# A two-layer image transformer on one core: the joint between the layers and the last steps are rebuilt

## The chip, the cores and the metric

The kernel runs on one core of one Trainium2 chip. A core has five engines that run side by side and wait for each other only through semaphores: PE (TensorE, matrix products into PSUM, with a separate queue for weight loads, PEld), DVE (VectorE), ACT (ScalarE), POOL (GpSimd) and SP (SyncE, which here issues most DMAs). The metric is the device time of one execution in microseconds (us); the median of several runs counts.

## The reference, cut to what matters

Two layers work on 256 tokens of `x` and 256 context tokens `ctx`, each of width 2048. Layer 0 is a Fourier branch, layer 1 an attention branch. Each layer normalises its input, modulates it, and adds a gated product back:

```python
for i in range(DEPTH):
    shift, scale, gate = split(silu(c) @ ada_w[i] + ada_b[i])
    h = rmsnorm(x, norm_g[i]) * (1 + scale) + shift
    hc = rmsnorm(xc, norm_g[i]) * (1 + scale_c) + shift_c
    y, yc = branch(h, hc)                 # Fourier, then attention
    x = x + gate * (y @ w_out[i])
    xc = xc + gate_c * (yc @ w_out[i])    # layer 0 only
return rmsnorm(x, final_g)
```

`rmsnorm(x, g)` is `x * rsqrt(mean(x*x) + 1e-6) * g`, the mean taken over the 2048 features of one token. So layer 1 can't begin before the squares of all features of layer 0's result are summed, and the output can't be written before those of layer 1's result are.

## The kernel before

Every large product is computed in three passes, because both operands are split into a high part (a rounded copy, made by ACT) and a low part (the difference, made by DVE): `split` (L61, L62) makes the parts, `half_split` applies it to half of a loaded weight block, and `mm3` (L74 to L76) issues high x high, high x low and low x high into the same PSUM bank. Weight blocks of 1 MB come in through three buffers (`raw`), and three pairs of split halves (`ws`) lie ready for PE. A scheduler orders each engine's instructions from a model of their times; `tc.issue_after(i)` only holds later instructions of the same engine behind instruction `i` in that order.

Within layer 0 the features lie on the partitions and the 512 tokens (256 of `x`, 256 of `ctx`) along the free axis. The last product of layer 0 runs over 32 steps, 16 for each half of the features, with all eight PSUM banks in use. In the last step of a half the banks are finished one by one, and `evac0` (L670 to L681) empties each: DVE adds the gated product to `x` (L674, two instructions), ACT squares the result (L677), and DVE adds the square to a running sum (L679). Of the 16 blocks of features the first 15 go into one sum and the last stays apart.

Then comes the joint, L705 to L736. PE turns the blocks by 128x128 transposes (`x1_turn`, L714), so that tokens lie on the partitions; ACT copies them out of PSUM (L716) and issues their DMA to a buffer in DRAM (L717), from which the end of the kernel fetches them. The sums over features are products with a column of ones (L731), two operands for each of four token blocks. `rsqrt` (L78 to L87) takes the root: DVE scales and adds epsilon (L82), GpSimd raises to the power of -0.5 (L83), and three DVE instructions do one Newton step (L84 to L86). `bcast_rows` (L97 to L101) spreads the four columns over all partitions with PE, and ACT copies the result out. Six turns stand ahead of the sums, two behind the broadcast. Layer 1 begins with the normalised, modulated blocks (L768 to L770) and the product with the key and value weights (`wkv`, L775), whose splits also go through L61 and L62.

At the end of layer 1 the output has four column blocks of 512 (`cb`) for two token blocks (`tb`). The last column block is computed with both token blocks side by side for five weight blocks; then token block 0 goes ahead with the last three, and token block 1's twelve steps are held back (`held`) and run last. `evac` (L1073 to L1081) multiplies a bank by the gate, adds `x` and has ACT square and sum it. `finish` (L1107 to L1119) adds the four partial sums, takes the root with `rsqrt`, scales the four column blocks (two on ACT, L1118, two on DVE, L1114 and L1116) and writes them out from SP (L1119).

## Time and profile before

| what | us |
|---|---|
| median of 3 runs | 1862.07 |
| lowest and highest | 1858.95 and 1866.89 |
| the profiled execution's own time | 1863.31 |
| its span in the profile | 1861.5 |
| last matmul of layer 0 ends, first matmul of layer 1 starts | 1029.98, 1040.88 |
| last matmul of the kernel ends | 1850.08 |

Times in the profile are counted from the start of the span. A timeline row gives start, duration, engine, line, operation, output and inputs with their shape, how many instructions are merged, and in brackets the idle time ahead of it with what ended it. Matmuls overlap each other, so the distance between two starts is their cost, not the duration of a row. One product with float32 operands stands as two passes in PE's counts.

### The profile page before, as it was taken

How to read it: one execution, taken by the hardware profiler on the slowest of the kernel's cores; microseconds unless marked ns; L12 is line 12 of the kernel's file. 1: busy time of each engine (PE TensorE's matmuls, PEld its weight loads, DVE VectorE, ACT ScalarE, POOL GpSimd, SP SyncE). 2: the span in 40 equal slices, each digit the busy share in tenths (PEclk: the TensorE clock that was granted, in tenths of full speed). 3: DMA queues.
4: the chain of work that ended last, by engine and by line, in shares of the span. 5: the costliest groups of instructions: out<-in, count | busy, mean ns of one | idle time of the engine just before them, and what ended most of it. 6: DMA issues, size and time to landing. Idle time of an engine off the chain costs nothing.

```text
span 1861.5 us, 26287 instructions
## 1 busy us (share of the span) xinstructions
PE 1824.5 (98%) x9953; PEld 1555.9 (84%) x9953; DVE 1412.0 (76%) x2406; ACT 976.5 (52%) x1713; POOL 158.7 (9%) x182
## 2 busy tenths in 40 slices
PE   7998999999999999999999999999999999999997
PEld 6658999998888888888888787888888888887886
DVE  5657999978897898578964825888878878887454
ACT  6445444444222243224222624888888888896343
POOL 0001000020000000000000001111220220300010
PEclk9999999999999999999999999999999999999999
DMA  7984565585766756654675324333333333434543
GB/s 314 362 355 148 196 209 197 188 287 204 299 259 228 277 197 256 257 216 165 228 265 215 114 94 147 123 135 132 118 120 130 136 117 133 159 136 181 186 176 136
DMA packets 63934, 362.74 MB, mean 195 GB/s; under 512 B 7744, under 2 KB 7888, under 8 KB 29504
## 3 DMA queue, kind: packets, MB, share of 16 engines
q1 hardware_dynamic: 52448, 326.67, 48.0%
q0 software_dynamic: 7472, 27.71, 4.0%
q10 hardware_dynamic: 3888, 6.69, 1.2%
q8 instruction: 78, 1.28, 0.3%
q14 instruction: 48, 0.39, 0.1%
HBM read 346.87 MB, written 14.16 MB: 194 GB/s over the span
## 4 chain that ended last, share of the span: by engine, by line
PE 93%; DVE 2%; DMA 2%; ACT 2%; issue 1%; POOL 0%; ACTq 0%; POOLq 0%; SPq 0%; DVEq 0%
PE ps L74 24%; PE ps L75 24%; PE ps L76 24%; PE ps L950 6%; PE ps L952 3%; PE ps L1006 3%; PE ps L1021 2%; PE ps L1020 2%; PE ps L986 2%; PE ps L987 1%; PE ps L254 1%; DMA m<-in_wm 1%; DMA raw<-in_awp 0%; DVE wl L62 0%; PE ps L236 0%
## 5 line engine op out<-in xcount | busy, mean ns | idle before, releaser
L61 ACT CAST wh<-raw 128x1024 fp32r<-128x1024 f32 x329 | 345.0, 1051 | 457.6 <-PE ps L75 348.6
L62 DVE TENSOR_TENSOR wl<-raw,wh 128x1024 fp32r<-128x1024 f32 x329 | 415.9, 1267 | 200.0 <-ACT wh L61 197.4
L75 PE MATMUL ps<-act,wh 128*128 128x512 f32 x928 | 361.0, 389 | 0.0
L74 PE MATMUL ps<-act,wh 128*128 128x512 f32 x928 | 357.9, 389 | 0.0
L76 PE MATMUL ps<-act,wl 128*128 128x512 f32 x928 | 356.6, 389 | 0.8 <-DVE wl L62 0.8
L76 PEld LDWEIGHTS ps<-act,wl 128*128 128x128 f32 x928 | 174.2, 188 | 37.3 <-DVE wl L62 1.2
L75 PEld LDWEIGHTS ps<-act,wh 128*128 128x128 f32 x928 | 174.2, 188 | 36.0
L74 PEld LDWEIGHTS ps<-act,wh 128*128 128x128 f32 x928 | 174.2, 188 | 35.9
L950 PE MATMUL ps<-h,wh 128*128 128x512 f32 x512 | 187.0, 400 | 0.0
L579 DVE CUSTOM_DVE_ANT_0 raw<-raw,cb 128x1024 f32<-128x1024 f32 x128 | 154.8, 1220 | 33.7 <-DMA raw<-in_adw 32.7
L579 DVE CUSTOM_DVE_ANT_0 junk<-raw,cb 128x1024 f32<-128x1024 f32 x96 | 117.1, 1220 | 29.4 <-DMA raw<-in_adw 16.1
L952 PE MATMUL ps<-h,wl 128*128 128x256 f32 x512 | 138.1, 280 | 0.0
L75 PE MATMUL ps<-wl,h 128*128 128x512 f32 x320 | 126.1, 394 | 1.5 <-DVE wl L62 1.5
L74 PE MATMUL ps<-wh,h 128*128 128x512 f32 x320 | 124.8, 398 | 0.2 <-ACT h L769 0.2
L76 PE MATMUL ps<-wh,h 128*128 128x512 f32 x320 | 124.5, 391 | 0.0
L950 PEld LDWEIGHTS ps<-h,wh 128*128 128x128 f32 x512 | 96.2, 188 | 19.0
L988 DVE CUSTOM_DVE_ANT_0 ps<-ps,mask,nsink 128x512 f32<-128x512 f32 x128 | 92.1, 754 | 12.3 <-PE ps L987 11.3
L991 ACT ACTIVATE p<-ps,mx 128x512 f32<-128x512 f32 x128 | 87.3, 687 | 24.8 <-DVE mx L988 24.2
L952 PEld LDWEIGHTS ps<-h,wl 128*128 128x128 f32 x512 | 96.8, 189 | 1.4
L62 DVE TENSOR_TENSOR pl<-ps,ph 128x512 fp32r<-128x512 f32 x128 | 83.7, 685 | 10.0 <-ACT ph L61 8.8
L996 ACT ACTIVATE p<-p,sm 128x512 f32<-128x512 f32 x128 | 85.4, 717 | 7.9 <-DVE sm L994 7.8
L75 PE MATMUL ps<-wl,ys 128*128 128x512 f32 x212 | 83.3, 393 | 0.0
(323 smaller groups left out, 3790.6 us busy)
## 6 DMA issues: line engine op xcount, KB each, us to landing
raw<-in_adw SPq DMA_DIRECT2D x64, 1024.0 KB, 5.1
raw<-in_wz SPq DMA_DIRECT2D x62, 1024.0 KB, 4.9
raw<-in_awp SPq DMA_DIRECT2D x32, 1024.0 KB, 8.0
raw<-in_wo SPq DMA_DIRECT2D x32, 1024.0 KB, 5.6
raw<-in_wq SPq DMA_DIRECT2D x32, 1024.0 KB, 4.8
raw<-in_wu SPq DMA_DIRECT2D x32, 1016.0 KB, 5.4
raw<-in_wo1b SPq DMA_DIRECT2D x16, 1024.0 KB, 4.9
act<-in_xT POOLq DMA_DIRECT2D x32, 256.0 KB, 5.2
```

What stands on the lines that cost most here:

```text
L61: S.copy(h, src)
L62: V.tensor_tensor(l, src, h.bitcast(F32), op=ALU.subtract)
L74: PE.matmul(o, wh, xh, start=start, stop=False)
L75: PE.matmul(o, wh, xl, start=False, stop=False)
L76: PE.matmul(o, wl, xh, start=False, stop=stop)
L579: V.tensor_tensor_reduce(junk if s == 0 and i < 3 else wf, wf, cb[:, s], 1.0, 0.0, ALU.mult, ALU.add, acc[:, i, kh, fg * 2 + f, s : s + 1])
L950: PE.matmul(o[0], wh[:, q], hx1[k], start=k == 0, stop=k == KT - 1)
L952: PE.matmul(o[0][:, 0:N], wl[:, q], hx1[k][:, 0:N], start=False, stop=False)
L988: V.tensor_tensor_reduce(o, o, mask[:, tb, :], -0.125, nsink[:, i : i + 1], ALU.add, ALU.min, mx[:, tb : tb + 1])
L991: S.activation(pt[:, tb, :], so[tb], AF.Exp, bias=mx[:, tb : tb + 1], scale=-1.0, accum_out=sm[:, tb : tb + 1])
L996: S.activation(pt[:, tb, :], pt[:, tb, :], AF.Copy, scale=sm[:, tb : tb + 1])
L1006: PE.transpose(o[:, (kt * 2 + tb) * P : (kt * 2 + tb + 1) * P], pt[:, tb, c : c + P], ident)
```

## The change

- The sums at the joint: the squares of the last two feature blocks of layer 0 are no longer added by DVE, but are two further operands of the product with ones. The square of block 13 is added behind the last evacuation. There are three operands for each of four token blocks instead of two.
- The root: `root` takes the square root on ACT and the reciprocal on DVE, then the same Newton step. `rsqrt` with GpSimd's power stays for layer 0's first norm. A one-element square root is issued at step 24 of layer 0's last product, and another one near the end, so that ACT holds its table.
- The turns: one group of two stands ahead of the sums, one between sums and broadcast, and two groups behind the broadcast; before it was three groups ahead and one behind.
- The first block of key and value weights: its first half is split at the last step of layer 0, its second half behind the first normalised block of layer 1.
- The end: the first three partial sums are added ahead of time (`known`), so that the root takes the last partial sum with the rest as its bias. Token block 1's last four steps are computed in two half banks of 256 columns, each emptied by itself (`part`); the full bank of its other steps is added to `x` meanwhile. The pieces are scaled and written in the order 2, 0, 3, 1, and the last piece of token block 1 is written from ACT's queue.

```diff
+    def root(pool, src, w, tag, bias=None):
+        v = pool.tile([P, w], F32, tag=tag + "v", name=tag + "v")
+        t = pool.tile([P, w], F32, tag=tag + "s", name=tag + "s")
+        r = pool.tile([P, w], F32, tag=tag + "r", name=tag + "r")
+        b = epsd if bias is None else bias
+        first = S.activation(t, src, AF.Sqrt, bias=b[:, 0:1], scale=1.0 / D).ins
+        V.tensor_scalar(v, src, 1.0 / D, EPS if bias is None else bias[:, 0:1], op0=ALU.mult, op1=ALU.add)
+        V.reciprocal(r, t)
+        newton(r, v, t)
+        return r, first
...
-            S.activation(t2, t, AF.Square)
-            if 0 < k < 15:
-                V.tensor_tensor(sqs[0], sqs[0], t2, op=ALU.add)
+            sq_end[0] = S.activation(t2, t, AF.Square).ins
+            if 0 < k < 14:
+                if k == 13:
+                    late.append(t2)
+                else:
+                    V.tensor_tensor(sqs[0], sqs[0], t2, op=ALU.add)
             else:
                 sqs.append(t2)
+            if k == 15:
+                with tc.issue_after(e):
+                    V.tensor_tensor(sqs[0], sqs[0], late[0], op=ALU.add)
...
+            if i == 31:
+                kv_raw = raw(a["wkv"][0])
+                kv_w = [half_split(kv_raw, 0)]
+            if i == 24:
+                S.activation(junk[:, 0:1], epsd, AF.Sqrt)
...
-    for c in range(3):
-        for tb in range(2):
-            x1_turn(tb, c)
+    turns(0, sq_end[0])
     r_bc1 = act()
     o = psum()
-    for t in range(4):
-        for i in range(2):
-            PE.matmul(o[:, t : t + 1], sqs[i][:, t * P : (t + 1) * P], ones[:, 0:1], start=i == 0, stop=i == 1)
-    r4 = rsqrt(const, o[:, 0:4], 4, "q")
-    bcast_rows(r4, r_bc1)
-    for tb in range(2):
-        x1_turn(tb, 3)
+    for i in (1, 2, 0):
+        for t in range(4):
+            with tc.issue_after(p_end[0]):
+                last = PE.matmul(o[:, t : t + 1], sqs[i][:, t * P : (t + 1) * P], ones[:, 0:1], start=i == 1 and t == 0, stop=i == 0 and t == 3).ins
+        p_end[0] = last
+    r4, rooted = root(const, o[:, 0:4], 4, "q")
+    turns(1, rooted, p_end[0])
+    with tc.issue_after(p_end[0]):
+        spread = bcast_rows(r4, r_bc1)
+    for c in (2, 3):
+        turns(c, p_end[0], spread)
...
+            def part(tb, j, o):
+                q, t, x = slice(1536 + j * 256, 1792 + j * 256), act()[:, 0:256], x2[tb][3][:, j * 256 : (j + 1) * 256]
+                V.tensor_tensor(t, o, gbc[:, q], op=ALU.mult)
+                V.tensor_tensor(x, x, t, op=ALU.add)
+                S.activation(t, x, AF.Square, accum_out=ss[:, 8 + j : 9 + j])
...
-            def finish(tb):
-                s2 = fp.tile([P, 1], F32, tag="s2", name="s2", bufs=2)
-                V.tensor_reduce(s2, ss[:, tb * 4 : tb * 4 + 4], axis=AX.X, op=ALU.add)
-                r = rsqrt(fp, s2, 1, f"f{tb}")
-                for c in (0, 3, 1, 2):
+            def finish(tb, col, base):
+                r, _ = root(fp, ss[:, col : col + 1], 1, f"f{tb}", base)
+                for c in (2, 0, 3, 1):
...
-                    nc.sync.dma_start(out[tb * P : (tb + 1) * P, c * 512 : (c + 1) * 512], t)
+                    (nc.scalar if tb and c == 1 else nc.sync).dma_start(out[tb * P : (tb + 1) * P, c * 512 : (c + 1) * 512], t)
...
-            finish(0)
-            for k, w in held:
+            base = [known(tb, 3, ss[:, tb * 4 : tb * 4 + 3], EPS) for tb in range(2)]
+            S.activation(ss[:, 9:10], epsd, AF.Sqrt)
+            finish(0, 3, base[0])
+            for k, w in held[:-4]:
                 step(k, 1, *w)
-            evac(1, 3, o[1])
-            finish(1)
+            t, x = act(), x2[1][3]
+            V.tensor_tensor(t, o[1], gbc[:, 1536:2048], op=ALU.mult)
+            V.tensor_tensor(x, x, t, op=ALU.add)
+            for j in range(2):
+                oh = psum()[:, 0:256]
+                for i, (k, (wh, wl)) in enumerate(held[-4:]):
+                    q = slice(j * 256, (j + 1) * 256)
+                    mm3(oh, yh[k][:, P : 2 * P], yh[k][:, N + P : 2 * N], wh[:, q], wl[:, q], i == 0, i == 3)
+                part(1, j, oh)
+                if j == 0:
+                    last = known(1, 1, ss[:, 8:9], base[1][:, 0:1])
+            finish(1, 9, last)
```

More of the change, by code (lines that the diff above doesn't have):

```diff
@@ L83, in rsqrt, with newton @@
         GP.tensor_tensor(r, v, mhalf[:, 0:w], op=ALU.pow)
+        newton(r, v, t)
+        return r
+    epsd = const.tile([P, 1], F32, name="epsd")
+    GP.memset(epsd, EPS)
+    def newton(r, v, t):
         V.tensor_tensor(t, r, r, op=ALU.mult)
@@ L86, in rsqrt @@
         V.scalar_tensor_tensor(r, t, 1.5, r, op0=ALU.add, op1=ALU.mult)
-        return r
+    def root(pool, src, w, tag, bias=None):
[6 more added lines that the diff above has]
+        V.reciprocal(r, t)
+        newton(r, v, t)
+        return r, first
     ident = const.tile([P, P], F32, name="ident")
@@ L100, in bcast_rows @@
             PE.matmul(o[:, t * P : (t + 1) * P], r4[:, t : t + 1].broadcast_to([P, P]), ident, start=True, stop=True)
-        S.copy(dst, o)
+        return S.copy(dst, o).ins
     gs0 = const.tile([P, KT, 2], F32, name="gs0")
@@ L673, in evac0 @@
                 q = slice(s * N, (s + 1) * N)
-                V.scalar_tensor_tensor(t[:, q], o[:, q], gt0[:, k, s : s + 1], t[:, q], op0=ALU.mult, op1=ALU.add)
+                e = V.scalar_tensor_tensor(t[:, q], o[:, q], gt0[:, k, s : s + 1], t[:, q], op0=ALU.mult, op1=ALU.add).ins
             x1.append(t)
             t2 = act()
-            S.activation(t2, t, AF.Square)
-            if 0 < k < 15:
-                V.tensor_tensor(sqs[0], sqs[0], t2, op=ALU.add)
+            sq_end[0] = S.activation(t2, t, AF.Square).ins
[4 more added lines that the diff above has]
+                    V.tensor_tensor(sqs[0], sqs[0], t2, op=ALU.add)
             else:
                 sqs.append(t2)
+            if k == 15:
+                with tc.issue_after(e):
+                    V.tensor_tensor(sqs[0], sqs[0], late[0], op=ALU.add)
+        late, sq_end = [], [None]
         xin = []
@@ L713, in x1_turn @@
         for j in range(4):
-            PE.transpose(o[:, j * P : (j + 1) * P], x1[c * 4 + j][:, tb * P : (tb + 1) * P], ident)
+            p_end[0] = PE.transpose(o[:, j * P : (j + 1) * P], x1[c * 4 + j][:, tb * P : (tb + 1) * P], ident).ins
         t = act()
@@ L717, in x1_turn, with turns @@
         nc.scalar.dma_start(x1d[tb, :, c * 512 : (c + 1) * 512], t)
+    def turns(c, *after):
+        with ExitStack() as es:
+            for i in after:
+                es.enter_context(tc.issue_after(i))
+            for tb in range(2):
+                x1_turn(tb, c)
+    p_end = [None]
     o = psum()
-    PE.transpose(o[0:KT, 0:P], gt1.rearrange("p k s -> p (k s)"), ident)
+    p_end[0] = PE.transpose(o[0:KT, 0:P], gt1.rearrange("p k s -> p (k s)"), ident).ins
     gr = const.tile([KT, P], F32, name="gr")
-    S.copy(gr, o[0:KT, 0:P])
+    with tc.issue_after(sq_end[0]):
+        S.copy(gr, o[0:KT, 0:P])
     nc.gpsimd.dma_start(gated.rearrange("o (k p) -> (o k) p", p=P), gr)
-    for c in range(3):
-        for tb in range(2):
-            x1_turn(tb, c)
+    turns(0, sq_end[0])
     r_bc1 = act()
     o = psum()
-    for t in range(4):
-        for i in range(2):
-            PE.matmul(o[:, t : t + 1], sqs[i][:, t * P : (t + 1) * P], ones[:, 0:1], start=i == 0, stop=i == 1)
-    r4 = rsqrt(const, o[:, 0:4], 4, "q")
-    bcast_rows(r4, r_bc1)
-    for tb in range(2):
-        x1_turn(tb, 3)
+    for i in (1, 2, 0):
[9 more added lines that the diff above has]
+        turns(c, p_end[0], spread)
     lay0.close()
@@ L769, in tile_dit @@
                     S.activation(h[:, 0:N], t[:, q], AF.Identity, bias=sh1[:, k, s : s + 1])
-                    V.scalar_tensor_tensor(h[:, N : 2 * N], t[:, q], sh1[:, k, s : s + 1], h[:, 0:N].bitcast(F32), op0=ALU.add, op1=ALU.subtract)
+                    hx_end = V.scalar_tensor_tensor(h[:, N : 2 * N], t[:, q], sh1[:, k, s : s + 1], h[:, 0:N].bitcast(F32), op0=ALU.add, op1=ALU.subtract).ins
+                if k == 0:
+                    hx_first = hx_end
                 hx1.append(hx)
@@ L774, in tile_dit @@
             for kg in range(8):
-                w = ws_split(raw(a["wkv"][kg]))
+                w = kv_w if kg == 0 else ws_split(raw(a["wkv"][kg]))
                 for j in range(2):
                     k = kg * 2 + j
+                    if k == 1:
+                        with tc.issue_after(hx_first):
+                            w.append(half_split(kv_raw, 1))
                     wh, wl = w[j]
@@ L1070, in tile_dit, with evac, known @@
             nc.gpsimd.dma_start(fg, a["fg"].broadcast_to([P, D]))
-            ss = fp.tile([P, 9], F32, name="ss")
-            def evac(tb, cb, o, c0=0, c1=512, col=None):
-                col = tb * 4 + cb if col is None else col
-                q, qx = slice(cb * 512 + c0, cb * 512 + c1), slice(c0, c1)
-                t, x = act()[:, 0 : c1 - c0], x2[tb][cb][:, qx]
-                V.tensor_tensor(t, o[:, qx], gbc[:, q], op=ALU.mult)
+            ss = fp.tile([P, 10], F32, name="ss")
+            def evac(tb, cb, o):
+                q, t, x = slice(cb * 512, (cb + 1) * 512), act(), x2[tb][cb]
+                V.tensor_tensor(t, o, gbc[:, q], op=ALU.mult)
                 V.tensor_tensor(x, x, t, op=ALU.add)
-                S.activation(t, x, AF.Square, accum_out=ss[:, col : col + 1])
+                S.activation(t, x, AF.Square, accum_out=ss[:, tb * 4 + cb : tb * 4 + cb + 1])
                 if cb < 3:
                     GP.tensor_tensor(x, x, fg[:, q], op=ALU.mult)
+            def part(tb, j, o):
+                q, t, x = slice(1536 + j * 256, 1792 + j * 256), act()[:, 0:256], x2[tb][3][:, j * 256 : (j + 1) * 256]
+                V.tensor_tensor(t, o, gbc[:, q], op=ALU.mult)
+                V.tensor_tensor(x, x, t, op=ALU.add)
+                S.activation(t, x, AF.Square, accum_out=ss[:, 8 + j : 9 + j])
+            def known(tb, w, src, b):
+                t = fp.tile([P, 1], F32, tag=f"kn{w}{tb}", name="kn")
+                if w > 1:
+                    V.tensor_reduce(t, src, axis=AX.X, op=ALU.add)
+                    src = t
+                u = fp.tile([P, 1], F32, tag=f"ku{w}{tb}", name="ku")
+                V.tensor_scalar(u, src, 1.0 / D, b, op0=ALU.mult, op1=ALU.add)
+                return u
             for k in range(12, NB, 2):
@@ L1104, in step @@
             def step(k, tb, wh, wl, q=slice(0, 512)):
-                mm3(o[tb][:, q], yh[k][:, tb * P : (tb + 1) * P], yh[k][:, N + tb * P : N + (tb + 1) * P], wh[:, q], wl[:, q], k == 0, k == NB - 1)
-            def finish(tb):
-                s2 = fp.tile([P, 1], F32, tag="s2", name="s2", bufs=2)
-                V.tensor_reduce(s2, ss[:, tb * 4 : tb * 4 + 4], axis=AX.X, op=ALU.add)
-                r = rsqrt(fp, s2, 1, f"f{tb}")
-                for c in (0, 3, 1, 2):
+                mm3(o[tb][:, q], yh[k][:, tb * P : (tb + 1) * P], yh[k][:, N + tb * P : N + (tb + 1) * P], wh[:, q], wl[:, q], k == 0, k == (NB - 1, NB - 5)[tb])
+            def finish(tb, col, base):
+                r, _ = root(fp, ss[:, col : col + 1], 1, f"f{tb}", base)
+                for c in (2, 0, 3, 1):
                     t = x2[tb][c]
```

## The prediction

> **What bounds the kernel now.** I read the page first, then the joint between the layers and the end engine by engine in the timeline, then the clock in the windows.

> ```profile
> PE 1824.5 (98%) x9953; PEld 1555.9 (84%) x9953; DVE 1412.0 (76%) x2406; ACT 976.5 (52%) x1713; POOL 158.7 (9%) x182
> PE 93%; DVE 2%; DMA 2%; ACT 2%; issue 1%; POOL 0%; ACTq 0%; POOLq 0%; SPq 0%; DVEq 0%
> ```

> TensorE is busy 98% of the 1861.5 us span and makes 93% of the chain that ended last. Only where TensorE waits or runs slowly can an edit of the other engines pay. The change touches two such places. The first is the joint; TensorE's rows there:

> ```profile
> 1029.59 0.39 PE L76 MATMUL ps<-act,wl 128*128 128x512 f32 x1
> 1029.92 2.78 PE L714 MATMUL ps<-ident,act 128*128 128x128 f32 x24
> 1032.89 1.95 PE L731 MATMUL ps<-ones,act 128*128 128x1 f32 x16 [0.19 <-DVE act L679]
> 1036.90 2.05 PE L100 MATMUL ps<-ident,qr 128*128 128x128 f32 x8 [2.06 <-DVE qr L86]
> 1038.73 1.91 PE L714 MATMUL ps<-ident,act 128*128 128x128 f32 x8
> 1040.88 0.80 PE L74 MATMUL ps<-wh,h 128*128 128x512 f32 x1 [0.23 <-ACT h L769]
> 1043.00 0.40 PE L75 MATMUL ps<-wl,h 128*128 128x512 f32 x1
> 1043.23 0.39 PE L74 MATMUL ps<-wh,h 128*128 128x512 f32 x1
> ```

> Layer 0 ends at 1029.98. 24 turns, the row sums, a pause of 2.06 us for the root, the broadcast and 8 more turns follow, and layer 1's matmuls begin at 1040.88. The matmul at 1043.00 is the sixth of them; at the later spacing of 0.23 it would have stood at 1040.88 + 5 x 0.23 = 1042.03. So the first five lose 0.97 us, and layer 1 in effect begins at 1041.85. The reason is the granted clock. Each row of the windows gives the stretch, its length, the busy time of PE, PEld, DVE, ACT and POOL, and then the clock, the DMA share and GB/s:

> ```profile
> 1138.30:1141.70 3.40, 1.95 (x9) 1.04 (x8) 2.55 (x2) 2.70 (x3) 3.27 (x3) 1.00 0.00 0
> 179.20:182.60 3.40, 1.47 (x12) 1.26 (x11) 3.40 (x4) 3.40 (x7) 0.00 (x0) 1.00 0.23 77
> 1032.50:1035.90 3.40, 2.15 (x18) 1.86 (x16) 1.64 (x3) 2.72 (x6) 0.77 (x1) 1.00 0.74 178
> 1035.90:1042.80 6.90, 5.67 (x21) 4.93 (x22) 3.52 (x11) 3.35 (x7) 0.26 (x1) 0.51 1.00 345
> ```

> The clock is halved for the 6.9 us from 1035.9 to 1042.8 (0.51). The stretch of 3.4 us before it holds 2.15 us of recorded work, but 1.95 of that are the one-column sums. The same length with 1.95 us of wide matmuls (1138.3) was not followed by a fall; one with 1.47 us (179.2) was. So I take the sums as hardly counting as work. The broadcast (1038.73 - 1036.90 = 1.83 us for 8 passes, 0.23 each) and the late turns run at half speed for this reason; the earlier turns take 2.78 / 24 = 0.116 each.

> [...]

> **The joint, part by part.** What feeds the sums and the root now:

> ```profile
> 1030.24 0.87 DVE L674 SCALAR_TENSOR_TENSOR act<-ps,gt,act 128x256 f32<-128x256 f32 x2
> 1031.02 1.21 DVE L62 TENSOR_TENSOR wl<-raw,wh 128x1024 fp32r<-128x1024 f32 x1
> 1032.15 0.68 DVE L679 TENSOR_TENSOR act<-act 128x512 f32<-128x512 f32 x1
> 1035.13 1.03 POOL L83 TENSOR_TENSOR qr<-qv,mhalf 128x4 f32<-128x4 f32 x1 [3.96 <-DVE qv L82]
> 1036.59 0.16 DVE L86 SCALAR_TENSOR_TENSOR qr<-qs,qr 128x4 f32<-128x4 f32 x1
> 1030.28 0.63 ACT L677 ACTIVATE act<-act 128x512 f32<-128x512 f32 x1
> 1038.98 0.58 ACT L101 COPY act<-ps 128x512 f32<-128x512 f32 x1 [3.76 <-PE ps L100]
> 1039.60 1.67 DVE L768 SCALAR_TENSOR_TENSOR ht<-act,gs 128x256 f32<-128x256 f32 x4 [2.85 <-ACT act L101]
> 1689.04 0.29 ACT L992 ACTIVATE es<-mx,sink 128x2 f32<-128x2 f32 x1
> ```

> *Sums.* Now they wait until 1032.83, because DVE does a weight split (L62) between the last evacuation and the last add. The change puts both splits behind, feeds the last two squares to TensorE by themselves, and leaves one add behind the last evacuation. That evacuation can begin when its bank is done, about 1030.0, and ends at 1030.9; its square ends 0.63 later, near 1031.55; the add of 0.68 ends near 1031.6. TensorE does one group of 8 turns first (1029.92 + 8 x 0.116 = 1030.85), then 12 products for 8: 24 passes for 16 at 1.95 / 16 = 0.122, so 2.93 us, unbroken from about 1030.95, when the square that starts at 1030.28 is there, to 1033.9. Now they end at 1034.84. Gain 0.95; the third operand costs 0.98, already in it.

> *Root.* From 1034.84 to 1036.75 is 1.91 us now, 1.03 of it GpSimd's power. Afterwards: an ACT square root (the nearest row is the 128x2 exponential with a bias, 0.29), a hop of 0.1, then five small DVE operations at 0.20 (0.16 and a gap), 1.0: together 1.4, ending at 1035.3. Gain 0.5. In the built order two copies of turns and their two DMA issues stand ahead of the root on ACT's queue; they are done by about 1033.1, before the sums end, so they cost nothing, and 0.3 if the first copy is late.

> *Turns.* Eight go into the pause, 1033.9 to 1034.85, which leaves 0.5 us of idling. Sixteen instead of eight stand behind the broadcast, ahead of layer 1. At full speed: broadcast 1035.4 + 0.93, turns 16 x 0.116 = 1.86, first matmul 1038.2. ACT's copy (0.58), DVE's first product (0.4), one copy of a turn and the first h (0.5 each) are ready by about 1038.1, so TensorE sets this point. But the sums are now 2.9 us long, and I hold that the clock falls once here too, somewhere from 1033.9 to 1036. With the gap nearly filled it should come back after one window of 3.4 us, not two. Half speed over 3.4 us of passes costs 1.0 to 1.7: 1039.2 to 1039.8, with layer 1 at full speed from its start. I take 1039.2. Gain 1041.85 - 1039.2 = 2.65; bounds 3.65 (no fall) and 1.15 (a fall within the sums, rival 2).

> *Splits.* The two moved splits (1.21 each) now stand among DVE's first layer-1 products. A step of layer 1 is 24 matmuls at 0.23, 5.5 us; DVE needs six products at 0.42 and one split, 3.7. The second split is first used some 27 matmuls in. No cost; without that cover it is at most 2.4.

> **The end.**

> ```profile
> 1849.69 0.39 PE L76 MATMUL ps<-wh,ys 128*128 128x512 f32 x1
> 1850.12 0.69 DVE L1077 TENSOR_TENSOR act<-ps,gbc 128x512 f32<-128x512 f32 x1 [3.43 <-PE ps L76]
> 1851.57 0.63 ACT L1079 ACTIVATE act<-act 128x512 f32<-128x512 f32 x1 [4.63 <-DVE act L1078]
> 1852.33 0.16 DVE L1109 TENSOR_REDUCE s<-ss 128x1 f32<-128x4 f32 x1 [0.79 <-ACT act L1079]
> 1852.75 0.56 POOL L83 TENSOR_TENSOR f1r<-f1v,mhalf 128x1 f32<-128x1 f32 x1 [7.82 <-DVE f1v L82]
> 1853.73 0.16 DVE L86 SCALAR_TENSOR_TENSOR f1r<-f1s,f1r 128x1 f32<-128x1 f32 x1
> 1854.59 0.48 DVE L1116 TENSOR_SCALAR act<-act,f1r 128x512 f32<-128x512 f32 x1
> 1854.67 0.33 SPq L1119 DMA_DIRECT2D out<-act  x1
> 1856.08 0.39 SPq L1119 DMA_DIRECT2D out<-act  x1
> GB/s 205 75 0 0 0 0 0 0 0 0 0 0 0 0 0 0 0 0 253 355 396 355 348 328 273 362 348 260 191 27 0 0 0 0 0 0 0 0 0 0
> 50.16 0.28 PE L75 MATMUL ps<-dl,xs 128*128 128x256 f32 x1
> 50.28 0.28 PE L76 MATMUL ps<-dh,xs 128*128 128x256 f32 x1
> 1700.33 0.42 DVE L1027 TENSOR_TENSOR ob<-ps,ot 64x256 f32<-64x256 f32 x1
> ```

> The GB/s row covers 1850 to 1862 in slices of 0.3 us. The last matmul ends at 1850.08, the root is there at 1853.89, 3.81 later. *Matmuls:* the last 12 of 512 columns become 24 of 256. Those follow each other at 0.12 (50.16, 50.28) against 0.23, so the work is equal; I charge 0.2 later. *Chain:* product and add of half width 0.42 + 0.04 each, one small DVE operation between them 0.2, square of half width about 0.41 (0.63 less 256 of its elements), reading the sum 0.1, root 0.3 with its hop, reciprocal 0.25, three small ones 0.6: 2.8. The product and add of the full bank and of the first half lie beside the 2.9 us of half-width matmuls. Gain 3.81 - 2.8 - 0.2 = 0.8. *Output:* the first DMA is issued 0.78 after the root now; with the DVE piece of 0.48 first it is 0.53. The four transfers keep the DMA engines full from 1855.4 to about 1858.9, so the earlier start counts, 0.25, and the fourth issue on ACT's queue does not. Gain in all 1.05; bounds 0.3 (half-width spacing 0.15 instead of 0.12) and 1.6.

> *Root table.* ACT must hold the table of the square root; the built order loads it in layer 0's last product, where ACT idles 4.38 us between splits (1013.47), and between attention and the end:

> ```profile
> 1013.47 1.05 ACT L61 CAST wh<-raw 128x1024 fp32r<-128x1024 f32 x1 [4.38 <-PE ps L75]
> 1170.24 1.28 ACT L991 ACT_TABLE_LOAD   x1
> 1706.10 1.05 ACT L61 CAST wh<-raw 128x1024 fp32r<-128x1024 f32 x1 [0.42 <-PE ps L75]
> 1709.13 1.05 ACT L61 CAST wh<-raw 128x1024 fp32r<-128x1024 f32 x1 [1.98 <-PE ps L75]
> ```

> It costs 1.28 and its small operation about 0.3. ACT's next two idle times there are 0.42 + 1.98 = 2.40, waiting for TensorE. No cost; if TensorE has to wait after all, at most 1.6.

> [...] The load row in this trace shows 1.28.

> **Sum.** 2.65 + 1.05 = 3.7 us. The profiled execution took 1863.31 (span 1861.5 and 1.81 around it), so it would take 1859.6; it lies 1.24 above the median of the three runs, 1862.07, so I forecast a median of 1858.4. Its case covers 1.15 + 0.3 to 3.65 + 1.6, a gain of 1.4 to 5.3.

> **The rivals.** 1: The clock does not fall in the joint, since eight turns break the idling. For it: the pause shrinks from 2.06 to 0.5. Against it: the sums grow from 1.95 to 2.9. The joint gives 3.65, the time is 1862.07 - 4.7 = 1857.4. 2: It falls already within the sums. Passes at 0.23 then end about 1 us later, root and broadcast follow, and layer 1 begins near 1040.7: gain 1.15 + 1.05, 1859.9. Against it: 0.9 us of full-width work at the start of that window. 3, the other side: the longer sums keep the clock low through the whole joint. 24 sum passes at 0.23 end at 1036.5, root 1037.9, broadcast 1039.7, sixteen turns 1043.4: 1.55 later than 1041.85, and the end's 1.05 does not cover it: 1862.6. It decides where the half clock begins before about 1031.5 and lasts beyond 1041; matmuls of full width run until 1029.98, which speaks against it. 4: the end gains nothing and the preloaded table stalls TensorE by 1.6: 1862.07 - 2.65 + 1.6 = 1861.0.

> [...]

> **How the numbers follow.** Chances: forecast 0.53, rival 1 0.15, rival 2 0.15, rival 3 0.09, rival 4 0.08. All lie within 1857.4 to 1862.6. The three runs scatter by 3.1 below and 4.8 above their median, more than the cases differ, and the median afterwards carries the same scatter. So the range is 1853.8 to 1863.8: the outer cases with most of this scatter. About 0.5%, 9.3 us, is what a measurement of this kernel can tell from no change; no case reaches it, and only scatter does: faster 0.06, same 0.90, slower 0.04.

> **What would show it.** The sums should end about 1 us sooner after layer 0's last matmul, the root's small chain should take 1.4, TensorE's pause before the broadcast should be about 0.5, the half clock should last about 3.4 us, and layer 1 should start some 9.2 us after layer 0's last matmul instead of 10.9. At the end the root should be there 3.0 after the last matmul and the first output be issued 0.5 later. A start of layer 1 later than 10.9 us, a wait for a split in its first steps, half-width matmuls spaced over 0.15, or a TensorE wait beside the table load would prove me wrong.

## The result

The changed kernel takes 1859.44 us (median of 22 runs, 1857.85 to 1861.79) against 1862.09 for the kernel before (22 runs, 1858.69 to 1866.89). The ratio is 0.9985, 95% interval 0.9978 to 0.9992: a gain of 2.8 us, between 1.5 and 4.1. Two later comparisons gave 0.9979 (0.9970 to 0.9988) and 0.9978 (0.9968 to 0.9987). The forecast was 1858.4 and a gain of 3.7, a ratio of 0.9980, which lies inside all three intervals. The profiled execution of the changed kernel took 1858.31, its span is 1856.5.

The page of the changed kernel, engines and chain:

```profile
PE 1822.3 (98%) x9973; PEld 1553.3 (84%) x9973; DVE 1414.7 (76%) x2415; ACT 981.4 (53%) x1722; POOL 156.7 (8%) x180
PE 93%; DVE 2%; DMA 2%; ACT 2%; issue 1%; SPq 0%; DVEq 0%; ACTq 0%
```

TensorE carries the same 93% of the chain; POOL and POOLq, GpSimd and its instruction queue, no longer stand in it. TensorE's timeline in the joint (start, duration, engine, line, operation, and in brackets the idle time ahead):

```profile
1028.96 0.39 PE L76 MATMUL ps<-act,wl 128*128 128x512 f32 x1
1029.29 1.04 PE L742 MATMUL ps<-ident,act 128*128 128x128 f32 x8
1030.16 2.84 PE L767 MATMUL ps<-ones,act 128*128 128x1 f32 x24
1032.87 1.07 PE L742 MATMUL ps<-ident,act 128*128 128x128 f32 x8
1034.32 1.57 PE L116 MATMUL ps<-ident,qr 128*128 128x128 f32 x8 [0.39 <-DVE qr L93]
1035.69 3.17 PE L742 MATMUL ps<-ident,act 128*128 128x128 f32 x16
1038.61 0.48 PE L74 MATMUL ps<-wh,h 128*128 128x512 f32 x1
1038.93 0.39 PE L75 MATMUL ps<-wl,h 128*128 128x512 f32 x1
```

Layer 0 ends at 1028.96 + 0.39 = 1029.35. The sums end 3.65 later (1033.00), the pause before the broadcast is 0.39, and layer 1 begins at 1038.61, 9.26 after layer 0's end; before, it was 10.90 with the first five matmuls slow. DVE's rows between the sums and the broadcast:

```profile
1030.18 0.68 DVE L703 TENSOR_TENSOR act<-act 128x512 f32<-128x512 f32 x1
1033.34 0.16 DVE L101 TENSOR_SCALAR qv<-ps 128x4 f32<-128x4 f32 x1 [2.48 <-ACT qs L100]
1034.01 0.16 DVE L93 SCALAR_TENSOR_TENSOR qr<-qs,qr 128x4 f32<-128x4 f32 x1
```

The last add of squares is done at 1030.86, where it was 1032.83, and the root is there at 1034.17, 1.17 after the sums. The windows (stretch, length, busy time of PE, PEld, DVE, ACT, POOL, then the clock, DMA share and GB/s) show one stretch of half clock, filled by TensorE to the end:

```profile
1031.43:1034.84 3.41, 3.02 (x27) 2.81 (x27) 0.73 (x5) 1.76 (x5) 0.44 (x1) 1.00 0.42 156
1034.84:1038.25 3.41, 3.41 (x19) 3.41 (x18) 1.70 (x5) 2.32 (x5) 0.00 (x0) 0.50 0.42 157
```

The end of the changed kernel, PE, DVE, ACT and the queues together:

```profile
1846.72 0.28 PE L76 MATMUL ps<-wh,ys 128*128 128x256 f32 x1
1847.04 0.42 DVE L1127 TENSOR_TENSOR act<-ps,gbc 128x256 f32<-128x256 f32 x1 [0.53 <-PE ps L76]
1847.51 0.42 DVE L1128 TENSOR_TENSOR act<-act 128x256 f32<-128x256 f32 x1
1847.96 0.42 ACT L1129 ACTIVATE act<-act 128x256 f32<-128x256 f32 x1 [0.90 <-DVE act L1128]
1848.50 0.29 ACT L100 ACTIVATE f1s<-ss,ku 128x1 f32<-128x1 f32 x1
1849.42 0.16 DVE L93 SCALAR_TENSOR_TENSOR f1r<-f1s,f1r 128x1 f32<-128x1 f32 x1
1850.20 1.31 SPq L1174 DMA_DIRECT2D out<-act  x3
1850.98 0.38 ACTq L1174 DMA_DIRECT2D out<-act  x1
```

The last matmul ends at 1847.00, the root is there at 1849.58, 2.58 later (before 3.81), and the span ends 9.50 after the last matmul (before 11.42).

### The profile page after: what moved, and what is told of

Same layout as the page of the kernel before. It is cut to its first block, busy times and chain, and to the rows that moved or that the text cites. A ratio compares the mean times of both kernels' runs of the same rounds, so it can differ in the third digit from the quotient of the medians.

```text
span 1856.5 us, 26344 instructions
## 1 busy us (share of the span) xinstructions
PE 1822.3 (98%) x9973; PEld 1553.3 (84%) x9973; DVE 1414.7 (76%) x2415; ACT 981.4 (53%) x1722; POOL 156.7 (8%) x180
## 3 DMA queue, kind: packets, MB, share of 16 engines
q0 software_dynamic: 7472, 27.71, 4.0%
q8 instruction: 78, 1.28, 0.3%
## 4 chain that ended last, share of the span: by engine, by line
PE 93%; DVE 2%; DMA 2%; ACT 2%; issue 1%; SPq 0%; DVEq 0%; ACTq 0%
PE ps L74 24%; PE ps L75 24%; PE ps L76 24%; PE ps L994 6%; PE ps L996 3%; PE ps L1050 3%; PE ps L1065 2%; PE ps L1064 2%; PE ps L1030 2%; PE ps L1031 2%; PE ps L270 1%; DMA raw<-in_awp 1%; DMA m<-in_wm 1%; DVE wl L62 0%; ACT wh L61 0%
## 5 line engine op out<-in xcount | busy, mean ns | idle before, releaser
L61 ACT CAST wh<-raw 128x1024 fp32r<-128x1024 f32 x329 | 345.5, 1053 | 453.7 <-PE ps L75 349.3
L62 DVE TENSOR_TENSOR wl<-raw,wh 128x1024 fp32r<-128x1024 f32 x329 | 416.4, 1268 | 205.4 <-ACT wh L61 202.8
L75 PE MATMUL ps<-act,wh 128*128 128x512 f32 x928 | 361.0, 389 | 0.0
L74 PE MATMUL ps<-act,wh 128*128 128x512 f32 x928 | 357.9, 389 | 0.0
L76 PE MATMUL ps<-act,wl 128*128 128x512 f32 x928 | 356.6, 389 | 0.8 <-DVE wl L62 0.8
L76 PEld LDWEIGHTS ps<-act,wl 128*128 128x128 f32 x928 | 174.2, 188 | 37.3 <-DVE wl L62 1.2
L75 PEld LDWEIGHTS ps<-act,wh 128*128 128x128 f32 x928 | 174.2, 188 | 36.1
L74 PEld LDWEIGHTS ps<-act,wh 128*128 128x128 f32 x928 | 174.2, 188 | 36.0
L75 PE MATMUL ps<-wl,h 128*128 128x512 f32 x320 | 125.6, 393 | 1.5 <-DVE wl L62 1.5
L76 PE MATMUL ps<-wh,h 128*128 128x512 f32 x320 | 124.4, 391 | 0.0
L74 PE MATMUL ps<-wh,h 128*128 128x512 f32 x320 | 123.7, 396 | 0.0
L62 DVE TENSOR_TENSOR pl<-ps,ph 128x512 fp32r<-128x512 f32 x128 | 83.7, 685 | 10.0 <-ACT ph L61 9.0
L75 PE MATMUL ps<-wl,ys 128*128 128x512 f32 (+1 forms) x216 | 84.0, 389 | 0.0
```

What stands on the lines that cost most here:

```text
L61: S.copy(h, src)
L62: V.tensor_tensor(l, src, h.bitcast(F32), op=ALU.subtract)
L74: PE.matmul(o, wh, xh, start=start, stop=False)
L75: PE.matmul(o, wh, xl, start=False, stop=False)
L76: PE.matmul(o, wl, xh, start=False, stop=stop)
```

## The experiments

Single times scatter by some 4 us, more than most of these edits are worth. Two sections of the trace repeat far better, and each kernel below is read by them: **joint section**, from the end of layer 0's last matmul to the end of the kernel's last matmul, and **end section**, from there to the end of the span. They are cut at rows like the first of the joint and of the end above; the span is given to a tenth, so an end section is good to 0.05. All traces together (us; "fall" and "layer 1" are counted from layer 0's last matmul; "idle in half clock" is TensorE's idle time inside the first 3.41 us of half clock):

| trace | clock falls | half clock lasts | idle in half clock | layer 1 begins | joint section | end section |
|---|---|---|---|---|---|---|
| before | 5.95 | 6.83 | 0.96 | 10.90 | 820.10 | 11.42 |
| before, 2nd | 4.79 | 6.83 | 2.06 | 10.91 | 819.52 | 11.42 |
| new end, old joint | 6.08 | 6.83 | 0.84 | 10.90 | 820.20 | 9.16 |
| after | 5.49 | 3.41 | 0 | 9.26 | 817.65 | 9.50 |
| after, 2nd | 5.12 | 3.41 | 0 | 9.26 | 817.56 | 9.47 |
| after, 3rd | none | - | - | 7.86 | 816.21 | 9.44 |
| new joint, old end | 5.37 | 3.41 | 0 | 9.26 | 817.65 | 11.45 |
| turns late, full bank | 5.49 | 3.41 | 0 | 10.14 | 818.52 | 9.90 |
| GpSimd's power | 5.01 | 6.83 | 0.71 | 10.83 | 819.61 | 10.59 |
| splits ahead, old order | 5.77 | 3.41 | 0 | 9.83 | 818.12 | 9.71 |
| wide sums | 9.84 | 3.41 | 0.17 | 10.01 | 819.68 | 9.20 |
| wide, exponential | none | - | - | 7.52 | 815.67 | 9.09 |
| wide, halved reciprocal | none | - | - | 7.53 | 815.73 | 9.41 |
| wide, two halves | none | - | - | 6.54 | 814.75 | 9.40 |

**1. The two kernels again, and each half of the change alone.** The third kernel is the changed one with everything from the tile of partial sums (`ss`) on taken from the kernel before:

```diff
-            ss = fp.tile([P, 10], F32, name="ss")
+            ss = fp.tile([P, 9], F32, name="ss")
...
-            finish(1, 9, last)
+            finish(1)
```

The fourth is the kernel before with that same part, and the new `root`, taken from the changed one:

```diff
-            ss = fp.tile([P, 9], F32, name="ss")
+            ss = fp.tile([P, 10], F32, name="ss")
...
-            finish(1)
+            finish(1, 9, last)
```

The kernel before:

> The kernel before, unchanged, for a second trace of its joint. Theory (the joint's gain is a matter of this kernel's own waits): layer 1 begins in effect 11.9 us after layer 0's last matmul again, within 0.3, and the half clock lasts two windows, 6.8 us. Rival (free-running clock windows): the time at which the clock falls moves against the sums and the root from run to run, the half clock may last one window or begin elsewhere, and the effective start lies anywhere from 9.9 to 11.9. Median 1862 by both.

The kernel after:

> The kernel after, unchanged, for a second trace of its joint. Theory: layer 1 begins 9.4 us after layer 0's last matmul, within 0.3, with one window of half clock (3.4 us). Rival (free-running windows): the fall comes elsewhere; if within the sums, 10.4 to 10.8 and the first matmuls of layer 1 at full clock; if only in the turns behind the broadcast, 9.0 to 10.0 with the first matmuls of layer 1 at half clock. Median 1859.4 by both.

The new joint alone:

> The new joint with the end of the kernel before (half banks, order of the outputs, ACT's root and preloaded table at the end are undone). Theory: the joint is worth 2.5 us and the end 1.9, and the two add: median 1.9 above the kernel after and 2.5 below the kernel before. From the last matmul to the end of the span 11.4 us as in the kernel before. Rival (the end gains nothing that lasts and the joint alone carries the measured 2.65): the median lies within 0.5 of the kernel after.

The new end alone:

> The joint of the kernel before with the new end (half banks, new order of the outputs, ACT's root there with its table loaded ahead). Theory: median 1.9 below the kernel before and 2.5 above the kernel after; 9.5 us from the last matmul to the end of the span, root 2.6 after the last matmul. Rival (only the joint pays): within 0.5 of the kernel before.

Measured, as ratios to the kernel before: after 0.9979 (0.9970 to 0.9988), the joint alone 0.9987 (0.9979 to 0.9996), the end alone 0.9989 (0.9979 to 0.9998), the kernel before itself 1.0001 (0.9993 to 1.0010). So both parts pay, 2.4 and 2.1 us against 3.9 together, and the intervals allow them to add. The traces say it more sharply: the joint section is 817.6 with the new joint whichever end follows, 819.5 to 820.2 with the old one; the end section is 11.4 with the old end and 9.2 to 9.5 with the new. Both rivals that gave the gain to one part alone are out. The rival in which the fall moves is partly right: it does move against the joint, by 1.3 us over three traces of the old one, and the joint section by 0.7.

**2. Parts of the change undone, two in each kernel, since joint and end lie 800 us apart.** The three kernels of this part and the first of the next ran once each, so they are read by their sections alone, against those of the kernel after. First, the eight turns back behind the broadcast, and the last four steps in the full bank:

```diff
-    turns(1, rooted, p_end[0])
-    for c in (2, 3):
+    for c in (1, 2, 3):
...
-            for k, w in held[:-4]:
+            for k, w in held:
...
+            evac(1, 3, o[1])
+            finish(1, 7, base[1])
```

> Two parts of the change undone, 800 us apart, each read in its own section of the trace. Joint: the eight turns that stand in the root's pause go behind the broadcast again. Theory (the turns are worth their own time, because the root takes as long with them as without): the broadcast starts 1.3 us after the sums as before, TensorE idles 1.2 instead of 0.4, and layer 1 begins 0.9 us later at full clock or up to 1.9 later at half clock, 10.2 to 11.2 us after layer 0's last matmul, with one window (3.4 us) of half clock. Rival (the turns are what keeps the half clock to one window): two windows, 6.8 us, and an effective start of 11.2 to 12.2. End: the last four steps fill the whole bank again, so product, add and square are 512 wide. Theory: root 3.3 us after the last matmul instead of 2.6, span end 10.2 after it instead of 9.5. Rival (half banks hide nothing): 2.6 and 9.5.

The pause grew from 0.39 to 1.31 and layer 1 begins 0.88 later; the joint section grows by 0.87. That is what eight turns at full clock take (8 x 0.116 = 0.93), and the half clock still lasts one stretch. TensorE's row:

```profile
1036.35 1.57 PE L116 MATMUL ps<-ident,qr 128*128 128x128 f32 x8 [1.31 <-DVE qr L93]
```

The clock fell at 1036.87, so the whole pause lies ahead of the fall. At the end the root came 3.32 after the last matmul as expected, 0.74 later, but the span's end only 0.40 later than in the kernel after (0.7 was expected): by the DMA packets the outputs took 3.27 us here and 3.70 there, and why isn't shown.

Second, GpSimd's power in place of ACT's square root and the reciprocal, at both places:

```diff
-    r4, rooted = root(const, o[:, 0:4], 4, "q")
-    turns(1, rooted, p_end[0])
+    r4 = rsqrt(const, o[:, 0:4], 4, "q")
+    turns(1, p_end[0])
...
-                r, _ = root(fp, ss[:, col : col + 1], 1, f"f{tb}", base)
+                r = rsqrt(fp, ss[:, col : col + 1], 1, f"f{tb}", base)
```

> The root alone undone at both places: GpSimd's power again instead of ACT's square root and the reciprocal. Joint, theory: from the end of the sums to the root 1.9 us instead of 1.2; the turns cover 0.9 of it, TensorE idles about 1.1, and layer 1 begins 0.7 later at full clock, up to 1.4 at half clock (10.0 to 10.8 us after layer 0's last matmul). Rival (the turns cover the root whoever computes it): within 0.2 of 9.3 to 9.4. End, theory: 0.45 later, root 3.0 after the last matmul and span end 9.95 after it. Rival: within 0.1 of 2.6 and 9.5.

The pause is 1.12 as expected, but the joint section grew by 1.96, where the theory allowed 0.7 to 1.4. TensorE's row, and the windows on the two stretches of half clock:

```profile
1036.22 2.05 PE L116 MATMUL ps<-ident,qr 128*128 128x128 f32 x8 [1.12 <-DVE qr L93]
```

```profile
1035.51:1038.92 3.41, 2.70 (x13) 2.73 (x14) 0.49 (x3) 1.17 (x2) 0.00 (x0) 0.50 0.41 154
1038.92:1042.33 3.41, 3.41 (x15) 3.22 (x15) 2.51 (x7) 3.03 (x7) 0.00 (x0) 0.50 0.20 77
```

Here the clock fell at 1035.51, inside the pause: 0.71 of it lies in the first stretch, TensorE is busy for 2.70 of 3.41, and a second stretch follows. A pause of 1.31 that ended before the fall (the kernel above) did not cost that. At the end, the root came 0.35 later as expected (0.45), but the span's end 1.09 later; the part on the end below shows why.

Third, the splits ahead of the joint again, and the outputs in the old order, all from SP:

```diff
-                kv_w = [half_split(kv_raw, 0)]
+                kv_w = ws_split(kv_raw)
...
-                for c in (2, 0, 3, 1):
+                for c in (0, 3, 1, 2):
```

> Joint: both weight splits of layer 1 stand ahead of the joint again, so that ACT's two casts (1.05 each) lie among the last squares. Theory: the square of the last block comes 1 to 2 us later, the sums end 1.0 later (4.6 us after layer 0's last matmul instead of 3.65), layer 1 begins 0.7 to 1.5 later. Rival (the sums are bound by TensorE's 24 passes): the sums end within 0.2 of 3.65. End: the four outputs in the old order and all on SP's queue. Theory: all of the difference between 7.6 and 6.9 us from root to span end comes from this, so 7.6 again. Rival (only the earlier first piece counts, 0.25): 7.15.

TensorE now waits in the middle of the sums for the last square, which stands behind ACT's second cast:

```profile
1033.45 1.95 PE L767 MATMUL ps<-ones,act 128*128 128x1 f32 x16 [0.41 <-ACT act L693]
```

The sums end 4.23 after layer 0, 0.58 later instead of the 1.0 expected, and layer 1 begins 0.57 later, a little under the theory's 0.7; the rival's 0.2 is out. At the end the rival's number is right: from root to span end 7.11, only 0.18 more than in the kernel after. Its reason is not: the last packet landed 4.99 after the root, 0.16 sooner than in the kernel after, and what follows the last packet took 2.1 instead of 1.8.

**3. Sums that count as work.** One-column passes seemed to count as idling for the clock: in the kernel after, the 3.41 us from 1031.43 held 3.02 us of recorded work, 1.57 of it one-column sums, and half clock followed. This kernel takes the same sums with a full matrix of ones; every partition then holds all the sums, and the broadcast and the small root go:

```diff
-        for t in range(4):
-            with tc.issue_after(p_end[0]):
-                last = PE.matmul(o[:, t : t + 1], sqs[i][:, t * P : (t + 1) * P], ones[:, 0:1], start=i == 1 and t == 0, stop=i == 0 and t == 3).ins
+        with tc.issue_after(p_end[0]):
+            last = PE.matmul(o, wide, sqs[i], start=i == 1, stop=i == 0).ins
...
+    rooted = S.activation(rt, o, AF.Sqrt, bias=epsd[:, 0:1], scale=1.0 / D).ins
+    V.reciprocal(r_bc1, rt)
```

> The kernel after with the 24 one-column sums replaced by three products of 512 columns with a matrix of ones, which give the sums already spread over all partitions; ACT takes the root of 128x512, DVE its reciprocal, and broadcast, small chain and Newton step go; the turns of groups 1 to 3 follow the sums at once. Theory (one-column passes count as idling for the clock, wide ones do not): the clock stays at 1.00 through the joint; if each wide sum takes about 0.9 us, the sums end 3.6 after layer 0's last matmul as now and TensorE goes on with 24 turns at 0.116, so layer 1 could begin 6.4 after layer 0's last matmul; ACT's six copies and the first products of DVE hold it to 7 to 8. Rival 1 (any joint of this shape loses a window): half clock 3.4 us, layer 1 at 8 to 10. Rival 2 (the root of 512 columns on ACT and DVE is the longer chain): TensorE waits over 1.5 us behind the turns.

The three wide sums took 2.65 (six passes of 0.44) and the clock stayed up through them, but rival 2 is right: the reciprocal of 512 columns is long, and TensorE waited 3.71 us for it. DVE's row:

```profile
1034.26 3.35 DVE L772 RECIPROCAL act<-act 128x512 f32<-128x512 f32 x1 [2.92 <-ACT act L771]
```

The clock fell only towards the end of that wait, at 1039.66, 9.84 after layer 0. Two versions shorten the chain behind the sums: a logarithm and an exponential on ACT, and the reciprocal in two halves. Neither has a Newton step. Both also put copies of turns behind the first modulated blocks (`h`) of layer 1, and the first of them gives three copies to DVE.

The kernel after, on the same chip:

> The kernel after again, to be compared with the two that follow on the same chip. Median 1859.3; from layer 0's last matmul to the last matmul of the kernel 817.6 us, 9.2 to 9.5 from there to the end of the span. A third trace of its joint: theory (one window of half clock, because TensorE does not idle inside it): one window again. Rival (chance of the position): two windows and 818.5 to 819.5.

```diff
+    S.activation(rt, o, AF.Ln, bias=epsd[:, 0:1], scale=1.0 / D)
+    S.activation(r_bc1, rt, AF.Exp, scale=-0.5)
```

> Wide sums again, without the long reciprocal: ACT takes the logarithm of 128x512 straight from the sums and then the exponential of minus half of it (one table load of 1.28 between them, the logarithm's loaded ahead); no Newton step, no broadcast; three of the six later copies of turns go to DVE, three on ACT behind the first two h. Theory (the clock stays up through wide sums, the path behind them sets layer 1): logarithm 0.7, load 1.3, exponential 0.6, product 0.5, h 0.5 behind the sums' end at 3.5, so layer 1 begins 7.1 us after layer 0's last matmul at full clock, 2.2 earlier than in the kernel after; section to the last matmul 815.4; median 2 lower than the kernel after. Rival 1 (the pause of 0.8 behind the turns lowers the clock all the same): 816.5 to 817.5, no faster than the kernel after. Rival 2 (banks or copies come late in layer 1's first steps): TensorE waits there for copies of turns, up to 1.

```diff
+    V.reciprocal(r_bc1[:, 0:N], rt[:, 0:N])
...
+                    if k == 0 and s == 1:
+                        with tc.issue_after(hx_end):
+                            V.reciprocal(r_bc1[:, q], rt[:, q])
```

> Wide sums with ACT's square root of 128x512 and DVE's reciprocal in two halves of 256 columns, the second behind the first h of layer 1; the last two copies of turns behind the first h on ACT. Theory: half a reciprocal 1.7; square root 0.7, reciprocal 1.7, product 0.5, h 0.5 behind the sums' end at 3.5: layer 1 begins 6.9 to 7.2 us after layer 0's last matmul, waits about 0.6 more for the second half, effective start 7.7; section to the last matmul 815.9 to 816.2, median 1.5 lower than the kernel after. Rival (pauses lower the clock in layer 1's first steps): 816.8 to 818.

The kernel after had no fall in its joint this time, which neither theory nor rival expected: 816.21. The two wide kernels also had none and are 0.5 shorter still; TensorE waits 1.2 us for the first `h` in both, and layer 1 begins some 0.4 later than expected. Ratios: after 0.9978 (0.9968 to 0.9987), exponential 0.9965 (0.9953 to 0.9977), halved reciprocal 0.9966 (0.9954 to 0.9978).

**4. The wide sums in two halves**, so that the first root runs beside the second half of the sums and the turns:

```diff
...
+    for s in range(2):
+        o = psum()
+        q = slice(s * N, (s + 1) * N)
+        for i in (1, 2, 0):
             with tc.issue_after(p_end[0]):
+                p_end[0] = PE.matmul(o[:, 0:N], wide, sqs[i][:, q], start=i == 1, stop=i == 0).ins
+        roots.append(S.activation(rt[:, q], o[:, 0:N], AF.Sqrt, bias=epsd[:, 0:1], scale=1.0 / D).ins)
+        if s == 0:
+            V.reciprocal(r_bc1[:, q], rt[:, q])
...
```

Copies of turns are put later here too.

> Wide sums again, in two halves of 256 columns, so that the root of the first half starts before the sums of the second: ACT's square root and DVE's reciprocal of 256 (1.75 measured) for the first half run while TensorE does the second half and the 24 turns; the second reciprocal stands behind the first product of layer 1. Theory (behind wide sums only the chain to the first h sets layer 1): first half of the sums done 2.4 us after layer 0's last matmul, square root 0.5, reciprocal 1.75, product 0.45, h 0.5: 5.6; TensorE's turns end at 6.3 and layer 1 begins there with no pause, 1.2 earlier than with one reciprocal per half behind all the sums; clock 1.00 through the joint; section to the last matmul 814.5; median about 1856. Rival 1 (the second reciprocal holds layer 1's first steps): 815.0 to 815.7. Rival 2 (the clock falls in some runs all the same): 816 to 817.5.

TensorE's rows in its joint, and the windows up to layer 1:

```profile
1031.00 1.03 PE L744 MATMUL ps<-ident,act 128*128 128x128 f32 x8
1031.91 3.19 PE L778 MATMUL ps<-act,wide 128*128 128x256 f32 x12
1034.94 2.78 PE L744 MATMUL ps<-ident,act 128*128 128x128 f32 x24
1037.59 0.50 PE L74 MATMUL ps<-wh,h 128*128 128x512 f32 x1
```

```profile
1031.83:1035.24 3.41, 3.31 (x17) 2.55 (x16) 1.62 (x3) 2.16 (x5) 2.14 (x4) 1.00 0.12 32
1035.24:1038.65 3.41, 3.41 (x28) 3.12 (x27) 3.37 (x5) 3.01 (x8) 0.00 (x0) 1.00 0.87 243
```

No pause, no fall: layer 1 begins 6.54 after layer 0, and the joint section is 814.75, 0.25 above the theory. The median is 1855.34 (five runs), the ratio to the kernel before 0.9962 (0.9948 to 0.9976). This is the shortest joint section and the lowest ratio here. The ratio's interval overlaps those of the other two wide kernels and, from 0.9968 to 0.9976, that of the kernel after; the joint section is shorter than in any of that kernel's traces (816.21 to 817.65).

## Why the prediction was right, and where it was not

**Sum.** In the joint the mechanism held. 2.65 was forecast, and the means of the traces, 819.94 with the old joint (three) and 817.27 with the new one (four), differ by 2.67. So close a match is partly luck: the three traces with one fall, the case that was forecast, give 2.32, and the fourth, without a fall, 3.73. For the end 1.05 was forecast and 2.0 came (11.43 against 9.39). The traces thus give 4.7, the three ratios 2.8 to 4.1, with upper ends of 4.1 to 6.0; 4.7 lies beyond the first interval and inside the two later ones. So the forecast of 3.7 lies near the measured gain although its end was undersized by half. Whether anything is lost in between isn't shown; the stretch ahead of the joint, which the change hardly touches, ends anywhere from 1028.80 to 1031.38 in these traces, and three or four traces need not have the mean position of the falls.

**Sums.** Expected 0.95 sooner, measured 4.86 - 3.65 = 1.21. They were unbroken, as said; one pass takes 2.71 / 24 = 0.113, not 0.122, and they start 0.81 after layer 0.

**Root and pause.** The small chain takes 1.17 instead of the 1.4 expected, TensorE's pause is 0.39 instead of 0.5. Sums and root together brought 0.5 more than was forecast.

**Clock.** "Once, somewhere from 1033.9 to 1036", 3.4 us: it fell once, at 1034.84, for 3.41. The 3.4 us can be read from the trace of the kernel before: half clock lasted 3.41 from 15.35 and from 182.60, with TensorE idle for 0.50 and 0 us of it, and 6.83 in the joint, idle for 0.96 of its first 3.41. The prediction allowed 1.0 to 1.7 for the stretch and took 1.0. Measured against the trace without a fall it cost 1.40 (layer 1 at 9.26 and 7.86), which took up most of the 0.5 gained above. So 9.26 against 9.2 owes something to two errors that largely cancel.

**Rivals.** Rival 1 (no fall, 0.15) occurred in one of four traces of the new joint. Its price was 3.65 for the joint; that trace gives 819.94 - 816.21 = 3.73. Rivals 2 and 3 did not occur in those four traces; rival 2 isn't excluded for other positions of the fall (an estimate stands in the last section).

**Splits and table.** No wait for a split in layer 1. The table is loaded in 1.28 beside TensorE's work, which has the same two waits near it (0.76 and 0.29 before, 0.77 and 0.29 after), so rival 4 is out. ACT's row:

```profile
1701.65 1.28 ACT L1200 ACT_TABLE_LOAD   x1
```

The operation behind the load starts 1.29 after the load does (1702.94), so nothing beyond the 1.28 shows.

**The end, the step that failed.** Its bounds were 0.3 to 1.6 and it brought 1.92 between the two profiled executions. The 0.2 charged for half-width matmuls was not there: they follow each other at 0.12 (from 1844.02 to 1846.72, 24 of them), so twelve steps cost 2.83 against 12 x 0.23 = 2.76. The chain took 2.58 instead of 2.8. The step that failed is the output's: 0.25 was counted because an earlier first issue should end the writes, and the span with them, that much sooner. Root to span end did fall, by 0.71 (7.64 to 6.93, by the unrounded ends of the traces), but not for this reason. The first issue came 0.16 sooner (0.62 after the root, against 0.78), the writes took 3.70 against 3.37, and by their packets the last one landed 5.15 after the root, against 4.98 before. The DMA view of the last 8.0 us, GB/s in slices of 0.2, shows where the time went. The kernel before, then GpSimd's power, splits ahead with the old order, and the kernel after:

```profile
GB/s 0 0 0 0 0 0 0 0 0 0 379 338 420 369 369 317 369 369 225 307 338 420 307 277 225 174 41 0 0 0 0 0 0 0 0 0 0 0 0 0
```

```profile
GB/s 0 0 0 0 0 0 0 0 123 399 348 410 348 399 307 400 277 256 307 379 430 389 287 164 21 0 0 0 0 0 0 0 0 0 0 0 0 0 0 0
```

```profile
GB/s 0 0 0 0 0 0 0 0 0 0 0 0 215 379 399 379 359 358 328 379 277 266 307 399 369 266 236 215 113 0 0 0 0 0 0 0 0 0 0 0
```

```profile
GB/s 0 0 0 0 0 0 0 0 0 0 0 0 102 399 369 389 338 420 276 420 287 246 297 369 389 389 287 215 41 31 20 0 0 0 0 0 0 0 0 0
```

All start their stream 1.4 to 1.6 after the root and move the same megabyte in 3.2 to 3.7. But what remains behind the last byte differs: 13 empty slices (2.6) before, 15 (3.0) with GpSimd's power and the fourth write on ACT's queue, 11 (2.2) with ACT's root and all writes on SP, 9 (1.8) after. So the gain lies behind the stream: with GpSimd's power as the last root the closing was 2.6 to 3.0 in four traces, without it 1.8 to 2.1 in the ten others.

The reason is GpSimd's last DRAIN, an instruction at the close of the program. Its rows in the kernel before and in the kernel after give how many there are, the shortest, median and longest in ns, and the first and last start:

```profile
L1247 POOLq DRAIN  x3: 46/93/8031, 1852.7 to 1861.3; - x3
```

```profile
L1313 POOLq DRAIN  x3: 46/102/12257, 1809.8 to 1856.2; - x3
```

Before, the long drain lasts from 1852.71 to 1860.74 and so ends 7.43 after the root's power (1853.31). SyncE's own closing drains were done at 1860.00, and the span ends 0.79 after GpSimd's. In all four traces with the power the drain ends 7.43 to 7.44 after it, and the span 0.78 to 0.79 after the drain, 7.64 to 7.65 after the root, whatever the order and the queues of the outputs. In the kernel after, GpSimd's last operation ends at 1814.62 and the drain behind it at 1822.06, long before the end. So in the kernel before, outputs issued sooner would not have ended the span any sooner: GpSimd held its end, and was done 0.74 later than SyncE. What the prediction missed is that taking GpSimd out of the last root takes this wait away.

## What to carry to other kernels

A short pause isn't priced by its length alone: look whether it lies inside a stretch of half clock, where 0.71 us of idling went with a second stretch of 3.41, or ahead of it, where 0.92 more of pause cost 0.88. Small one-column products between large ones did not keep the clock up here (half clock followed 3.41 us with 3.02 of recorded work, 1.57 of it such sums); done at full width, with the result already spread, they left it at 1.00 and saved the broadcast, as soon as the long reciprocal behind them (3.35 us) was cut in two (1.75 each) and put beside other work. Look also at what closes the program: an operation on GpSimd in the last steps held the span's end by 0.74 here, through its closing drain, which ended 7.43 after that operation. And where runs scatter by more than an edit is worth, read its own section of the trace: it repeated within some 0.1 us wherever the clock behaved alike.

## What the runs showed of the hardware

*What counts as work.* Two windows held the same 3.02 us of recorded work: the one from 1031.43 of the kernel after (above), which ended in a fall, and one of its third trace, which did not. The window of the third trace, then of the sums alone (their line only, PE and PEld) in the kernel after, then in the third trace:

```profile
1032.71:1036.12 3.41, 3.02 (x27) 2.81 (x28) 0.73 (x5) 1.55 (x4) 0.00 (x0) 1.00 0.51 192
```

```profile
1031.43:1034.84 3.41, 1.57 (x15) 1.49 (x14) 1.00 0.42 156
```

```profile
1032.71:1036.12 3.41, 1.10 (x10) 1.01 (x10) 1.00 0.51 192
```

Without the one-column sums they hold 1.45 and 1.92. So a window fell at 1.45 of 3.41 and not at 1.92, which agrees with the two windows of the prediction (1.47 fell, 1.95 did not). The other windows of the grid bear it out. In all fourteen traces, counting TensorE's recorded time without the sums in every window that begins at full clock and later than 9 us into the execution, all 43 with at most 1.55 us were followed by half clock and none of the 7472 with 1.60 or more. With the sums counted no such line can be drawn: a window with 3.21 us fell. Before 9 us, windows with less did not fall (one with 0.23 us from 4.01 in the kernel after).

Moving the grid over the rows of these traces, with a fall assumed behind every window below that line of 1.55 to 1.60, gives an estimate for other positions. The old joint falls at every position. The new one falls at about 87% of them, between 2.7 and 5.6 us after layer 0's last matmul, and at a third of these inside the sums, which is rival 2 and was not met. The two shortened wide kernels and the one in two halves fall at none, since their poorest window holds 2.2 us.

Half clock ended after windows of the joint with 0 to 0.17 us of idling (six traces) and went on after 0.71 to 2.06 (four). The stretches near the start of the executions narrow this: it ended after 0.53 (wide sums, from 15.66) and went on after 0.67 (wide, two halves, from 14.66).

*The reciprocal.* DVE's reciprocal of 128x512 takes 3.35 us and of 128x256 1.75, 6.5 to 6.8 ns a column, where an addition of 128x512 takes 0.68.
